# Three value tiles first in the neighbourhood attention, and the gate's mix beside the key products in the RWKV layer

## The chip, the cores and the metric

The kernel runs on one core of one Trainium2 chip. The metric is the device time of one execution in microseconds (us). Before the change, three runs took 2551.04, 2552.61 and 2557.27 us; the median is 2552.61.

## What is computed

The reference is a diffusion transformer of four layers with two streams: 256 latent tokens `x` and 256 context tokens `xc`, each token 1024 wide. Each layer is modulation, a mixer, a gated residual with a layer norm, and an MLP with squared ReLU. The mixers are attention with axial rotary positions (layers 0 and 3), neighbourhood attention (layer 1) and a bidirectional RWKV-7 (layer 2). Cut to the two places that matter here:

```python
# layer 1, neighbourhood attention
q, k, v = jnp.split(u @ wqkv, 3, axis=-1)        # u: latent or context tokens
# layer 2, RWKV
xx = _token_shift_centred(h)
xr, xw, xk, xv, xa, xg = [h + xx * p['mu'][j] for j in range(6)]
r = (xr @ p['wr']).reshape(hs)
k = xk @ p['wk']
v = (xv @ p['wv']).reshape(hs)
w = p['w0'] + tanh(xw @ w1) @ w2                 # shortened
a = sigmoid(p['a0'] + (xa @ a1) @ a2)            # shortened
g = jax.nn.sigmoid(xg @ p['g1']) @ p['g2']
...
return (y * g) @ p['wo']
```

So the RWKV layer mixes `h` six times with its neighbours, once for each of six products. The gate `g` is used only at the layer's end.

## The kernel before

**Products.** Activations lie with the feature on the partitions, in eight tiles of 128 features by 512 tokens (context and latent tokens beside each other). A product of full precision is made of three matmuls on rounded halves: high weight by high activation (L430), high weight by low activation (L431), low weight by high activation (L432); for products that have the tokens on the partitions the same three are L479 to L481. A product of one weight tile (128 output features) is thus 8 x 3 = 24 matmuls of 512 columns. An activation is split by ACT, which rounds it to the high half, and DVE, which subtracts (`split`, L425).

**Weights.** `Stream` brings weight tiles of 512 KB in the order of the list `PLAN`: SP loads `wr`, ACT rounds it to `wh`, and DVE subtracts to get `wl` (L280), which I call the residue. `W.next` checks that the tile asked for is the next of `PLAN`, so a product that moves has to move in `PLAN` too. `W.depth` says how many tiles are split ahead. The engines work in order, and a scheduler with priorities decides the order of each engine's instructions before the launch.

**Neighbourhood attention** (`natten`). The layer's input for the latent tokens is late: its norm needs the end of the layer before (`centre`, `finish`). `opening` therefore runs some passes on the context tokens alone first, with `centre` and `finish` issued among them (`at`). Here the passes are two value tiles, `values(0)` and `values(1)`; their weights are kept, and `together` (L856 to L858) then does both tiles for the latent tokens. Tiles 2 and 3 follow for all tokens. In `finish`, ACT takes the square root `rs` of the variance product, DVE scales `zc`, ACT makes `hx`, and `split` makes the pair `h`.

**RWKV.** `mixer(j)` makes the mixed tiles of one of the six products when asked for, each by one DVE instruction (L1025) and one split. `low` is a product on eight such tiles, made as it goes. The order of the program is: the products for `r`, `low` of `w1`, of `a1` and of `g1` (whose sigmoid goes into `sig`), and then eight key products; three tiles of the next mix are asked for ahead of each `low`'s last instruction (`PM` = 3). From key 0 on, preparatory steps for the recurrent units run beside the products: `wps` (`gate_products`, L1177), `kss` (L1192), and in the end `AR` and `BK` on DVE, from which 32 small matmuls (`tps`, L1263) make the triangles. DVE and DMAs carry these to POOL, which solves them (L1290, L1292), and the result R (L1313) is needed by PE at L1322. Between the keys and R the values' products run.

Of the kernel before, what the change touches and what calls it, by code (L numbers as in the profile page):

```python
# [12 lines left out]
AF = mybir.ActivationFunctionType  # L13
# [23 lines left out]
def plan():  # L37

    g = []
    for i in range(DEPTH):  # L40
        if i % 3 == 0:
            a = i // 3
            g += [("att_wqkv", a, "T", 0, n) for n in (8, 9)]
            g += [("att_wqkv", a, "V", kh, 5) for kh in range(2)]
            g += [("att_wqkv", a, "T", 0, n) for n in range(8)]
            g += [("att_wo", a, "T", 0, n) for n in range(8)]
        elif i % 3 == 1:
            g += [("na_wqkv", 0, "V", kh, 8 + j) for j in range(4) for kh in range(2)]
            for c in range(8):
                g += [("na_wqkv", 0, "T", 0, 8 + c), ("na_wqkv", 0, "T", 0, c)]  # L50
            g += [("na_wo", 0, "T", 0, n) for n in range(8)]
        else:
            g += [("rw_wr", 0, "T", 0, n) for n in range(8)]
            g += [("rw_w1", 0, "L", 0, 0), ("rw_a1", 0, "L", 0, 0), ("rw_g1", 0, "T", 0, 0)]
            g += [("rw_wk", 0, "T", 0, n) for n in range(8)]
            g += [("rw_wv", 0, "V", kh, j) for j in range(4) for kh in range(2)]
            g += [("rw_wo", 0, "T", 0, n) for n in range(8)]
        for w, q in MLP_ORDER:
            if w == "1":
                g += [("mlp_w1", i, "T", 0, 8 * q + n) for n in range(8)]  # L60
            else:
                g += [("mlp_w2", i, "T", q, n) for n in range(8)]
    return g
# [130 lines left out]
def dit_kernel(ctx: ExitStack, tc: tile.TileContext, places, t_in, out, layers=DEPTH):  # L194
    nc = tc.nc
    pe, dve, pool, sp = nc.tensor, nc.vector, nc.gpsimd, nc.sync
    act = InOrder(tc, nc.scalar)
# [23 lines left out]
    def bank(p, n, name):  # L221
        return p.tile([128, 512], F32, tag="b", name=name)[:, 0:n]
# [69 lines left out]
    W = Stream()  # L292
# [168 lines left out]
        mm3(ps, w, h[KC - 1], 0, 512, KC - 1, False, True)  # L461
        return ps

    def gemm_v(h, parts, toks):

        out = []
        for x, t in enumerate(toks):
            if x % 2 == 0:
                ps_b = bank(ps_mm, 512, "vps")
            out.append(ps_b[:, (x % 2) * 256:(x % 2) * 256 + 256])  # L470
        for kh in range(2):
            wh, wl = parts[kh]() if callable(parts[kh]) else parts[kh]
            for x, t in enumerate(toks):
                ps = out[x]
                for k in range(4):
                    c = kh * 4 + k
                    sh, sl = h[c][:, 0, t * 128:(t + 1) * 128], h[c][:, 1, t * 128:(t + 1) * 128]
                    first, last = c == 0 and x % 2 == 0, c == 7 and x % 2 == 1
                    pe.matmul(ps, lhsT=sh, rhs=wh[:, k * 256:(k + 1) * 256], start=first, stop=False)  # L479
                    pe.matmul(ps, lhsT=sh, rhs=wl[:, k * 256:(k + 1) * 256], start=False, stop=False)  # L480
                    pe.matmul(ps, lhsT=sl, rhs=wh[:, k * 256:(k + 1) * 256], start=False, stop=last)  # L481
        return out
# [348 lines left out]
    def natten(i, h, gate, nrm, begun, ends):  # L831
        V = [k4("nV") for _ in range(4)]
        kept = {}

        def values(j, toks):
            def part(kh):
                def go():
                    if (j, kh) not in kept:
                        kept[j, kh] = W.next("na_wqkv", 0, "V", kh, 8 + j)
                    return kept[j, kh]  # L840
                return go

            def go():
                for t, ps in zip(toks, gemm_v(h(), [part(0), part(1)], toks)):
                    act.copy(out=V[t][:, j * 256:(j + 1) * 256], in_=ps)
            return go

        def together():

            ps = [bank(ps_mm, 512, "vps").rearrange("p (t d) -> p t d", t=2) for _ in range(2)]  # L850
            for c in range(KC):
                for j in range(2):
                    vh, vl = (w[:, (c % 4) * 256:(c % 4) * 256 + 256] for w in kept[j, c // 4])
                    for t in range(2):
                        sh, sl = (h()[c][:, y, t * 128:(t + 1) * 128] for y in range(2))
                        pe.matmul(ps[j][:, t], lhsT=sh, rhs=vh, start=c == 0 and t == 0, stop=False)  # L856
                        pe.matmul(ps[j][:, t], lhsT=sh, rhs=vl, start=False, stop=False)
                        pe.matmul(ps[j][:, t], lhsT=sl, rhs=vh, start=False, stop=c == 7 and t == 1)  # L858
            for j in range(2):
                for t in range(2):  # L860
                    act.copy(out=V[t][:, j * 256:(j + 1) * 256], in_=ps[j][:, t])

        opening(begun, (0, 1), lambda cnd: [values(0, TOKS[1]), values(1, TOKS[1])] if cnd else [together], at=(0, 0))
        kept.clear()
        values(2, range(4))()
        values(3, range(4))()
        kept.clear()
        h = h()
# [93 lines left out]
    def rwkv(i, hx, gate, nrm, begun, ends):  # L962
# [143 lines left out]
        made[1](PM)  # L1106
        act.activation(out=lora[:, 0], in_=ps, func=AF.Tanh)
        ps = low("rw_a1", "L", made[1])
        made[2](PM)
        act.copy(out=lora[:, 1], in_=ps)  # L1110
        ps = low("rw_g1", "T", made[2])
        made[3](PM)
        act.activation(out=sig, in_=ps, func=AF.Sigmoid)
        m = made[3](KC)
        W.limit = PLAN.index(("rw_wo", 0, "T", 0, 0))
        W.depth = 2

        def keys(c):
            def go():
                if c == 9:  # L1120
                    W.depth = 1
                keep(c, 1, gemm(W.next("rw_wk", 0, "T", 0, c), m, ALL))
                if c == 7:
                    made[4](PM)
            return go
# [36 lines left out]
        def prep(c):  # L1162
# [5 lines left out]
            def gate_products():  # L1168
                q["sg"], q["ag"] = [], []
                wa = sml.tile([128, 2, 128], F32, tag="wa", bufs=2, name="wa")  # L1170
                sp.dma_start(out=wa, in_=t_in["rws"][c, :, 0:2])
                todo = []
                for x, (key, bias) in enumerate((("sg", "w0"), ("ag", "a0"))):
                    for d in range(2):
                        sl = slice(64 * d, 64 * d + 64)
                        ps = bank(ps_s if x else ps_mm, 512, "wps")
                        pe.matmul(ps, lhsT=wa[sl, x], rhs=lora[sl, x], start=True, stop=True)  # L1177
                        t = tmp(512 if x else 520, key)
                        q[key].append(t)
                        dst = t  # L1180
                        if x == 0:
                            dve.memset(b8(t)[:, :, 0:1], 0.0)
                            dst, ps = b8(t)[:, :, 1:65], b8(ps)
                        todo.append(dict(out=dst, in_=ps, bias=C(bias, "rw")[:, d, c:c + 1]))
                sigmoids(todo)
            out.append(gate_products)

            def unit_k():
# [610 lines left out]
```

## Time and profile before

| | |
|---|---|
| median of three runs | 2552.61 us |
| the profiled execution itself | 2547.62 us |
| its span, first to last instruction | 2545.2 us |
| PE busy | 2448.7 us, 96% |
| DVE busy | 1664.0 us, 65% |
| ACT busy | 1188.7 us, 47% |
| POOL busy | 209.2 us, 8% |
| mean granted clock | 0.987 |

The profiled execution is 5.0 us shorter than the median. Times in the rows below count from its first instruction. "PEclk" is the clock granted to PE as a share of its full 2.4 GHz. In a timeline, consecutive equal instructions are one row with their count (x3), and the bracket at a row's end is the idle time just before it on the engine, with the instruction that ended it.

### The profile page before, as it was taken

How to read it: one execution, taken by the hardware profiler on the slowest of the kernel's cores; microseconds unless marked ns; L12 is line 12 of the kernel's file. 1: busy time of each engine (PE TensorE's matmuls, PEld its weight loads, DVE VectorE, ACT ScalarE, POOL GpSimd, SP SyncE). 2: the span in 40 equal slices, each digit the busy share in tenths (PEclk: the TensorE clock that was granted, in tenths of full speed). 3: DMA queues.
4: the chain of work that ended last, by engine and by line, in shares of the span. 5: the costliest groups of instructions: out<-in, count | busy, mean ns of one | idle time of the engine just before them, and what ended most of it. 6: DMA issues, size and time to landing. Idle time of an engine off the chain costs nothing. (4 is left out here: it accounts for less than half of the span.)

```text
span 2545.2 us, 53184 instructions
## 1 busy us (share of the span) xinstructions
PE 2448.7 (96%) x22337; PEld 2085.8 (82%) x22337; DVE 1664.0 (65%) x3087; ACT 1188.7 (47%) x2226; POOL 209.2 (8%) x383
## 2 busy tenths in 40 slices
PE   8999999999999999999889799899999999998998
PEld 5779888889766988888867677778898888998997
DVE  4567777775566777787786565673567663766555
ACT  3555443244566543334555444544362343465644
POOL 0002000002000110000202112211020000121000
PEclk9999999999999999999999999999999999999999
DMA  8432556642211245665132311210336654223553
GB/s 337 166 127 75 182 189 192 207 157 88 69 55 58 88 152 182 207 205 176 60 112 77 80 28 33 41 20 15 143 107 216 206 184 126 93 68 115 175 184 98
DMA packets 158415, 324.11 MB, mean 127 GB/s; under 512 B 77393, under 2 KB 80993, under 8 KB 158177
## 3 DMA queue, kind: packets, MB, share of 16 engines
q1 hardware_dynamic: 158176, 320.73, 39.8%
q8 instruction: 175, 2.87, 0.5%
q14 instruction: 64, 0.52, 0.1%
HBM read 310.71 MB, written 9.97 MB: 126 GB/s over the span
## 5 line engine op out<-in xcount | busy, mean ns | idle before, releaser
L430 PE MATMUL mm<-h,wh 128*128 128x512 f32 (+1 forms) x1472 | 515.5, 351 | 6.1 <-ACT h L180 4.7
L432 PE MATMUL mm<-h,wl 128*128 128x512 f32 (+1 forms) x1472 | 511.6, 348 | 1.1 <-DVE wl L280 1.1
L280 DVE TENSOR_TENSOR wl<-wr,wh 128x1024 fp32r<-128x1024 f32 x363 | 442.7, 1227 | 103.5 <-ACT wh L180 77.9
L431 PE MATMUL mm<-h,wh 128*128 128x512 f32 (+1 forms) x1472 | 510.0, 347 | 0.3 <-DVE h L425 0.2
L180 ACT CAST wh<-wr 128x1024 fp32r<-128x1024 f32 x363 | 373.8, 1049 | 261.7 <-DVE wl L280 89.2
L430 PE MATMUL mm<-f,wh 128*128 128x512 f32 (+1 forms) x1168 | 397.6, 340 | 0.0
L432 PE MATMUL mm<-f,wl 128*128 128x512 f32 (+1 forms) x1168 | 397.6, 340 | 0.0
L431 PE MATMUL mm<-f,wh 128*128 128x512 f32 (+1 forms) x1168 | 397.0, 340 | 0.0
L430 PEld LDWEIGHTS mm<-h,wh 128*128 128x128 f32 x1472 | 279.4, 190 | 50.0 <-issue 8.8
L432 PEld LDWEIGHTS mm<-h,wl 128*128 128x128 f32 x1472 | 279.8, 190 | 37.1 <-issue 3.0
L431 PEld LDWEIGHTS mm<-h,wh 128*128 128x128 f32 x1472 | 279.8, 190 | 34.5 <-issue 2.8
L431 PEld LDWEIGHTS mm<-f,wh 128*128 128x128 f32 x1168 | 221.6, 190 | 24.7
L430 PEld LDWEIGHTS mm<-f,wh 128*128 128x128 f32 x1168 | 221.6, 190 | 24.5
L432 PEld LDWEIGHTS mm<-f,wl 128*128 128x128 f32 x1168 | 221.6, 190 | 24.2
L180 ACT ACTIVATE relu<-mm 128x512 f32<-128x512 f32 (+1 forms) x146 | 72.5, 497 | 360.4 <-PE mm L432 360.3
L425 DVE TENSOR_TENSOR f<-sqr,f 128x512 fp32r<-128x512 f32 (+1 forms) x146 | 82.4, 567 | 210.4 <-ACT f L180 210.4
L492 DVE SCALAR_TENSOR_TENSOR x<-mm,gate,x 128x256 f32<-128x256 f32 x280 | 127.3, 480 | 128.5 <-PE mm L432 128.3
L544 POOL TENSOR_SCALAR x<-zc,cs 128x256 f32<-128x256 f32 x88 | 86.0, 990 | 1302.9 <-DVE zc L575 1302.9
L387 DVE SCALAR_TENSOR_TENSOR mwt<-mwt,srow 128x1024 f32<-128x1024 f32 x144 | 175.8, 1221 | 8.3 <-DMA mwt<-in_mwr_dram 6.9
L387 DVE SCALAR_TENSOR_TENSOR mpr<-mwt,srow 128x1024 f32<-128x1024 f32 x112 | 136.7, 1220 | 0.5
L430 PE MATMUL mm<-o,wh 128*128 128x256 f32 (+1 forms) x400 | 120.1, 302 | 0.3 <-ACT o L180 0.2
L432 PE MATMUL mm<-o,wl 128*128 128x256 f32 (+1 forms) x400 | 119.9, 300 | 0.1
(292 smaller groups left out, 4317.9 us busy)
## 6 DMA issues: line engine op xcount, KB each, us to landing
wr<-in_gw_dram SPq DMA_DIRECT2D x363, 512.0 KB, 3.7
mwt<-in_mwr_dram SPq DMA_DIRECT2D x144, 512.0 KB, 4.3
mwt<-in_mw_dram SPq DMA_DIRECT2D x48, 512.0 KB, 5.4
srow<-srow_d SPq DMA_DIRECT2D x6, 512.0 KB, 4.1
nab<-in_nab_dram SPq DMA_DIRECT2D x8, 384.0 KB, 3.3
rk<-rk_d SPq DMA_DIRECT2D x6, 512.0 KB, 5.1
rk_d<-rkp SPq DMA_DIRECT2D x10, 256.0 KB, 2.2
x<-in_xt_dram SPq DMA_DIRECT2D x4, 512.0 KB, 10.2
```

The costliest lines, as they stand in the source:

```text
L180: x = f(*args, **kw)
L280: self.lo[self.done % len(self.lo)].tensor_tensor(out=lo, in0=t, in1=hi.bitcast(F32), op=ALU.subtract)
L387: dve.scalar_tensor_tensor(out=to, in0=t, scalar=1.0, in1=rw_["s"][cnd], op0=ALU.mult, op1=ALU.mult, accum_out=m[:, cnd, r * 8 + c:r * 8 + ...
L425: eng.tensor_tensor(out=dst[:, 1, a:b], in0=src, in1=dst[:, 0, a:b].bitcast(F32), op=ALU.subtract)
L430: pe.matmul(ps, lhsT=st, rhs=hl[:, 0, a:b], start=first, stop=False)
L431: pe.matmul(ps, lhsT=st, rhs=hl[:, 1, a:b], start=False, stop=False)
L432: pe.matmul(ps, lhsT=wl[:, c * 128:(c + 1) * 128], rhs=hl[:, 0, a:b], start=False, stop=last)
L492: dve.scalar_tensor_tensor(out=xc(c)[:, a:b], in0=ps[:, a - base:b - base], scalar=gate[:, cnd, c:c + 1], in1=xc(c)[:, a:b], op0=ALU.mult, ...
L544: (eng or dve).tensor_scalar(out=dst, in0=src, scalar1=ca, scalar2=cb, op0=ALU.mult, op1=ALU.add)
```

## The change

In the neighbourhood attention three value tiles in place of two are done first for the context tokens, the norm's `finish` comes behind the second, and `together` does three tiles. Their accumulators come from the pools in `OPEN`. Tile 3 alone remains for all tokens at once.

In the RWKV layer the weight of `g1` moves in `PLAN` from ahead of key 0 to behind key 3. The eight mixed tiles of the gate are asked for two at a time behind the key products 0 to 3, and `low` of `g1` comes behind key 3. Its result is copied, and the sigmoid is taken in place in the batch of unit 1's sigmoids. Ahead of key 0, the key's mix follows `low` of `a1`. The condition `c == 9` that goes was never true.

```diff
--- before.py
+++ after.py
@@ -51,8 +51,10 @@
             g += [("na_wo", 0, "T", 0, n) for n in range(8)]
         else:
             g += [("rw_wr", 0, "T", 0, n) for n in range(8)]
-            g += [("rw_w1", 0, "L", 0, 0), ("rw_a1", 0, "L", 0, 0), ("rw_g1", 0, "T", 0, 0)]
-            g += [("rw_wk", 0, "T", 0, n) for n in range(8)]
+            g += [("rw_w1", 0, "L", 0, 0), ("rw_a1", 0, "L", 0, 0)]
+            g += [("rw_wk", 0, "T", 0, n) for n in range(4)]
+            g += [("rw_g1", 0, "T", 0, 0)]
+            g += [("rw_wk", 0, "T", 0, n) for n in range(4, 8)]
             g += [("rw_wv", 0, "V", kh, j) for j in range(4) for kh in range(2)]
             g += [("rw_wo", 0, "T", 0, n) for n in range(8)]
         for w, q in MLP_ORDER:
@@ -461,12 +463,12 @@
         mm3(ps, w, h[KC - 1], 0, 512, KC - 1, False, True)
         return ps
 
-    def gemm_v(h, parts, toks):
+    def gemm_v(h, parts, toks, pool=None):
 
         out = []
         for x, t in enumerate(toks):
             if x % 2 == 0:
-                ps_b = bank(ps_mm, 512, "vps")
+                ps_b = bank(pool or ps_mm, 512, "vps")
             out.append(ps_b[:, (x % 2) * 256:(x % 2) * 256 + 256])
         for kh in range(2):
             wh, wl = parts[kh]() if callable(parts[kh]) else parts[kh]
@@ -832,7 +834,7 @@
         V = [k4("nV") for _ in range(4)]
         kept = {}
 
-        def values(j, toks):
+        def values(j, toks, pool=None):
             def part(kh):
                 def go():
                     if (j, kh) not in kept:
@@ -841,28 +843,27 @@
                 return go
 
             def go():
-                for t, ps in zip(toks, gemm_v(h(), [part(0), part(1)], toks)):
+                for t, ps in zip(toks, gemm_v(h(), [part(0), part(1)], toks, pool)):
                     act.copy(out=V[t][:, j * 256:(j + 1) * 256], in_=ps)
             return go
 
         def together():
 
-            ps = [bank(ps_mm, 512, "vps").rearrange("p (t d) -> p t d", t=2) for _ in range(2)]
+            ps = [bank(ps_mm, 512, "vps").rearrange("p (t d) -> p t d", t=2) for _ in range(3)]
             for c in range(KC):
-                for j in range(2):
+                for j in range(3):
                     vh, vl = (w[:, (c % 4) * 256:(c % 4) * 256 + 256] for w in kept[j, c // 4])
                     for t in range(2):
                         sh, sl = (h()[c][:, y, t * 128:(t + 1) * 128] for y in range(2))
                         pe.matmul(ps[j][:, t], lhsT=sh, rhs=vh, start=c == 0 and t == 0, stop=False)
                         pe.matmul(ps[j][:, t], lhsT=sh, rhs=vl, start=False, stop=False)
                         pe.matmul(ps[j][:, t], lhsT=sl, rhs=vh, start=False, stop=c == 7 and t == 1)
-            for j in range(2):
+            for j in range(3):
                 for t in range(2):
                     act.copy(out=V[t][:, j * 256:(j + 1) * 256], in_=ps[j][:, t])
 
-        opening(begun, (0, 1), lambda cnd: [values(0, TOKS[1]), values(1, TOKS[1])] if cnd else [together], at=(0, 0))
+        opening(begun, (0, 1), lambda cnd: [values(j, TOKS[1], OPEN[j + 2]) for j in range(3)] if cnd else [together], at=(0, 1))
         kept.clear()
-        values(2, range(4))()
         values(3, range(4))()
         kept.clear()
         h = h()
@@ -1106,20 +1107,19 @@
         made[1](PM)
         act.activation(out=lora[:, 0], in_=ps, func=AF.Tanh)
         ps = low("rw_a1", "L", made[1])
-        made[2](PM)
+        made[3](PM)
         act.copy(out=lora[:, 1], in_=ps)
-        ps = low("rw_g1", "T", made[2])
-        made[3](PM)
-        act.activation(out=sig, in_=ps, func=AF.Sigmoid)
         m = made[3](KC)
         W.limit = PLAN.index(("rw_wo", 0, "T", 0, 0))
         W.depth = 2
 
         def keys(c):
             def go():
-                if c == 9:
-                    W.depth = 1
                 keep(c, 1, gemm(W.next("rw_wk", 0, "T", 0, c), m, ALL))
+                if c < 4:
+                    made[2](2 * c + 2)
+                if c == 3:
+                    act.copy(out=sig, in_=low("rw_g1", "T", made[2]))
                 if c == 7:
                     made[4](PM)
             return go
@@ -1182,7 +1182,7 @@
                             dve.memset(b8(t)[:, :, 0:1], 0.0)
                             dst, ps = b8(t)[:, :, 1:65], b8(ps)
                         todo.append(dict(out=dst, in_=ps, bias=C(bias, "rw")[:, d, c:c + 1]))
-                sigmoids(todo)
+                sigmoids(todo + ([dict(out=sig, in_=sig)] if c == 1 else []))
             out.append(gate_products)
 
             def unit_k():
```

On PE, at the end of the context tokens' second pass, the order before is this (`vps` are value products, `pvar` is the variance product on which `finish` waits; L856 and L857 are `together`):

```order
L481 MATMUL vps_5692<-wh_5589,h_5461 128x256
L479 MATMUL vps_5692<-wh_5589,h_5467 128x256
L480 MATMUL vps_5692<-wl_5590,h_5467 128x256
L481 MATMUL vps_5692<-wh_5589,h_5467 128x256
L537 MATMUL pvar_5643<-s1_5623,cs_83 128x256
L856 MATMUL vps_5755<-wh_5243,h_5422 128x256
L857 MATMUL vps_5755<-wl_5244,h_5422 128x256
L856 MATMUL vps_5756<-wh_5559,h_5422 128x256
L857 MATMUL vps_5756<-wl_5560,h_5422 128x256
L479 MATMUL vps_5857<-wh_5693,h_5422 128x256
```

After the change (lines count two more there) a third pass of 48 products stands in between, and `pvar` in it:

```order
L482 MATMUL vps_5643<-wl_5590,h_5467 128x256
L483 MATMUL vps_5643<-wh_5589,h_5467 128x256
L481 MATMUL vps_5755<-wh_5644,h_5422 128x256
L482 MATMUL vps_5755<-wl_5645,h_5422 128x256
L483 MATMUL vps_5755<-wh_5644,h_5422 128x256
L481 MATMUL vps_5755<-wh_5644,h_5428 128x256
L539 MATMUL pvar_5706<-s1_5623,cs_83 128x256
L482 MATMUL vps_5755<-wl_5645,h_5428 128x256
L483 MATMUL vps_5755<-wh_5644,h_5428 128x256
```

What moved is `pvar`, four products into the new pass, and `together`, which now begins behind all of it.

On PE in the RWKV layer, the end of `a1` (`low_12158`) was followed by the gate's product (`low_12230`):

```order
L430 MATMUL low_12158<-mh_12200,wh_12090 128x512
L431 MATMUL low_12158<-mh_12200,wh_12090 128x512
L432 MATMUL low_12158<-mh_12200,wl_12091 128x512
L430 MATMUL low_12230<-mh_12208,wh_12152 128x512
L431 MATMUL low_12230<-mh_12208,wh_12152 128x512
L432 MATMUL low_12230<-mh_12208,wl_12153 128x512
L1177 MATMUL wps_12408<-lora_11513,wa_12398 128x512
L430 MATMUL low_12230<-mh_12213,wh_12152 128x512
L1177 MATMUL wps_12411<-lora_11513,wa_12398 128x512
```

It is now followed by key 0 (`mm_12268`), which runs on the next mixed tiles:

```order
L433 MATMUL low_12158<-mh_12200,wh_12090 128x512
L434 MATMUL low_12158<-mh_12200,wl_12091 128x512
L432 MATMUL mm_12268<-mh_12208,wh_12152 128x512
L433 MATMUL mm_12268<-mh_12208,wh_12152 128x512
L434 MATMUL mm_12268<-mh_12208,wl_12153 128x512
L1177 MATMUL wps_12356<-lora_11513,wa_12346 128x512
L432 MATMUL mm_12268<-mh_12213,wh_12152 128x512
L1177 MATMUL wps_12359<-lora_11513,wa_12346 128x512
```

The gate's product (`low_12475`) stands behind key 3 (`mm_12431`), with a `wps` of unit 1 in it:

```order
L432 MATMUL mm_12431<-mh_12244,wh_12376 128x512
L433 MATMUL mm_12431<-mh_12244,wh_12376 128x512
L434 MATMUL mm_12431<-mh_12244,wl_12377 128x512
L432 MATMUL low_12475<-mh_12294,wh_12425 128x512
L433 MATMUL low_12475<-mh_12294,wh_12425 128x512
L1177 MATMUL wps_12770<-lora_11513,wa_12760 128x512
L434 MATMUL low_12475<-mh_12294,wl_12426 128x512
L432 MATMUL low_12475<-mh_12299,wh_12425 128x512
L433 MATMUL low_12475<-mh_12299,wh_12425 128x512
```

So 24 products went from ahead of key 0 to ahead of key 4, and the two `wps` of unit 0 that stood among them are in key 0.

On DVE, the last key tiles before the change (`mh_12306` to `mh_12316`) are followed by residues of weights and by unit 0:

```order
L1025 SCALAR_TENSOR_TENSOR mix_12317<-xx_11524,cs_rw_11511,x_117 128x512
L425 TENSOR_TENSOR mh_12306<-mix_12307,mh_12306 128x512
L425 TENSOR_TENSOR mh_12311<-mix_12312,mh_12311 128x512
L425 TENSOR_TENSOR mh_12316<-mix_12317,mh_12316 128x512
L1530 MEMSET resets_12321 128x520
L280 TENSOR_TENSOR wl_12335<-wr_12156,wh_12334 128x1024
L1531 MEMSET resets_12321 128x8
L1182 MEMSET sg_12402 128x8
L1182 MEMSET sg_12406 128x8
L280 TENSOR_TENSOR wl_12367<-wr_12228,wh_12366 128x1024
L1203 SCALAR_TENSOR_TENSOR sg_12402<-resets_12321,sg_12402 128x520
L280 TENSOR_TENSOR wl_12429<-wr_12338,wh_12428 128x1024
```

After it (`mh_12244` is the last key tile) the gate's tiles come between them, beginning with `mix_12295` and `mh_12294`:

```order
L427 TENSOR_TENSOR mh_12239<-mix_12240,mh_12239 128x512
L1026 SCALAR_TENSOR_TENSOR mix_12245<-xx_11524,cs_rw_11511,x_117 128x512
L1530 MEMSET resets_12249 128x520
L1026 SCALAR_TENSOR_TENSOR mix_12295<-xx_11521,cs_rw_11511,x_114 128x512
L427 TENSOR_TENSOR mh_12244<-mix_12245,mh_12244 128x512
L1531 MEMSET resets_12249 128x8
L1026 SCALAR_TENSOR_TENSOR mix_12300<-xx_11521,cs_rw_11511,x_114 128x512
L282 TENSOR_TENSOR wl_12263<-wr_12094,wh_12262 128x1024
L427 TENSOR_TENSOR mh_12294<-mix_12295,mh_12294 128x512
L427 TENSOR_TENSOR mh_12299<-mix_12300,mh_12299 128x512
L1026 SCALAR_TENSOR_TENSOR mix_12337<-xx_11522,cs_rw_11511,x_115 128x512
L282 TENSOR_TENSOR wl_12305<-wr_12156,wh_12304 128x1024
```

What moved are the gate's mixes and splits: they stood ahead of the key tiles and now stand among the residues for keys 1 to 4.

## Rows read from the trace of the kernel before

**Rows 1.** The page, busy time of each engine, share of the span, instructions.
```profile
PE 2448.7 (96%) x22337; PEld 2085.8 (82%) x22337; DVE 1664.0 (65%) x3087; ACT 1188.7 (47%) x2226; POOL 209.2 (8%) x383
```

**Rows 2.** Busy time by stretch around the attention's values.
```profile
core 0: us, PE busy (x) PEld busy (x) DVE busy (x) ACT busy (x) POOL busy (x), PEclk, DMA share, GB/s
600.00:610.00 10.00, 6.53 (x37) 5.76 (x36) 7.63 (x14) 8.02 (x20) 6.42 (x7) 0.83 0.16 54
610.00:620.00 10.00, 10.00 (x86) 10.00 (x85) 1.08 (x3) 2.02 (x7) 1.10 (x2) 1.00 0.42 118
```

**Rows 3.** Timeline of PE from 600 to 642: start, duration, what, idle before.
```profile
600.51 0.28 PE L481 MATMUL vps<-wh,h 128*128 128x256 f32 x1
601.10 0.70 PE L537 MATMUL pvar<-s,cs 128*128 128x256 f32 x2 [0.31 <-DVE s L530]
604.96 0.39 PE L856 MATMUL vps<-wh,h 128*128 128x256 f32 x1 [3.16 <-ACT h L180]
...
606.21 0.42 PE L856 MATMUL vps<-wh,h 128*128 128x256 f32 x1
606.42 0.42 PE L857 MATMUL vps<-wl,h 128*128 128x256 f32 x1
...
641.31 0.40 PE L430 MATMUL mm<-h,wh 128*128 128x512 f32 x1
```

**Rows 4.** Timeline of ACT in the same stretch.
```profile
603.52 1.09 ACT L180 ACTIVATE hx<-zc,ab 128x256 f32<-128x256 f32 x2 [0.76 <-DVE zc L575]
604.52 0.70 ACT L180 CAST h<-hx 128x256 fp32r<-128x256 f32 x2
```

**Rows 5.** Timeline of DVE in the same stretch.
```profile
600.96 1.22 DVE L280 TENSOR_TENSOR wl<-wr,wh 128x1024 fp32r<-128x1024 f32 x1
...
605.20 0.95 DVE L425 TENSOR_TENSOR h<-hx,h 128x256 fp32r<-128x256 f32 x2
```

**Rows 6.** Busy time by stretch (columns as in rows 2), around key 0.
```profile
1320.00:1330.00 10.00, 6.87 (x23) 3.90 (x23) 10.00 (x17) 7.61 (x12) 0.00 (x0) 1.00 0.39 113
```

**Rows 7.** Timeline of DVE, key tiles and unit 0.
```profile
1318.99 2.08 DVE L1025 SCALAR_TENSOR_TENSOR mix<-xx,cs_rw,x 128x512 f32<-128x512 f32 x3
...
1322.79 2.08 DVE L1025 SCALAR_TENSOR_TENSOR mix<-xx,cs_rw,x 128x512 f32<-128x512 f32 x3
...
1328.57 1.90 DVE L425 TENSOR_TENSOR mh<-mix,mh 128x512 fp32r<-128x512 f32 x3
...
1354.18 0.69 DVE L1220 TENSOR_TENSOR BK<-BK,cc 128x512 f32<-128x512 f32 x1
```

**Rows 8.** Timeline of PE, keys, first triangles and the solver's result.
```profile
1323.13 0.39 PE L431 MATMUL mm<-mh,wh 128*128 128x512 f32 x1
1323.35 0.39 PE L432 MATMUL mm<-mh,wl 128*128 128x512 f32 x1
...
1331.04 0.39 PE L432 MATMUL mm<-mh,wl 128*128 128x512 f32 x1
...
1361.98 1.15 PE L1263 MATMUL tps<-AR,BK 64*64 64x64 f32 x32
...
1406.13 0.74 PE L1322 MATMUL pa<-R,TT 32*32 32x32 f32 x34 [3.91 <-DVE R L1313]
```

**Rows 9.** Timeline of POOL, the solver: first, two between, last.
```profile
1380.61 0.40 POOL L1290 TENSOR_TENSOR xw<-lane 128x15 f32<-128x15 f32 x1 [31.59 <-DMA lane<-dr]
...
1390.30 0.32 POOL L1292 TENSOR_TENSOR lane<-lane,xw 128x64 f32<-128x64 f32 x1
...
1392.62 1.16 POOL L1292 TENSOR_TENSOR lane<-lane,xw 128x55 f32<-128x55 f32 x1
...
1398.04 0.23 POOL L1292 TENSOR_TENSOR lane<-lane,xw 128x15 f32<-128x15 f32 x1
```

**Rows 10.** Timeline of DVE beside the solver.
```profile
1392.25 2.62 DVE L280 TENSOR_TENSOR wl<-wr,wh 128x1024 fp32r<-128x1024 f32 x2
```

**Rows 11.** Timeline of ACT before the solver.
```profile
1377.74 1.28 ACT L180 ACT_TABLE_LOAD   x1
```

## The prediction

> **What bounds the kernel now.** I read the page's busy times first: the tensor engine (PE) is busy for 2448.7 of 2545.2 us [rows 1], so only stretches in which it idles, or runs at the lower clock, can give time back; the number of matmuls is the same after the change. After it I read the table of busy time by stretch, and then the timelines of the two stages touched, engine by engine.
>
> In the neighbourhood attention's value stage PE is busy 6.53 of the 10 us from 600 to 610, at a granted clock of 0.83, and 10.00 of 10 in the next ten [rows 2]. The gap is one wait: the last value product of the context tokens starts at 600.51, the variance product at 601.10, and the first product of `together` at 604.96, after 3.16 us on ACT's `h` [rows 3]. The chain behind that wait is the square root on ACT, the scaled `zc` on DVE, `hx` at 603.52, the rounded `h` at 604.52 [rows 4], and the low half of `h` at 605.20 [rows 5]. After the gap PE's matmuls of 256 columns stand 0.21 us apart (606.21, 606.42 [rows 3]) in place of 0.12 (86 in 10 us [rows 2]): 1.2 instead of 2.4 GHz, by the mean of 0.83 for some 3.4 of the ten us.
>
> In the RWKV layer the owner changes. From 1320 to 1330 DVE is busy 10.00 of 10 and PE 6.87 [rows 6]: DVE makes mixed tiles in groups of three, 2.08 us of mixes and 1.90 of splits, and a group starts 3.8 us after the one before (1318.99, 1322.79) [rows 7]. PE waits for each group. The last group's splits start at 1328.57 and end at 1330.47 [rows 7], and the last matmul of key 0 starts at 1331.04 [rows 8]. Here a tile less on DVE ahead of key 0 is time.
>
> Farther on PE waits 3.91 us for R, the solver's result, at 1406.13 [rows 8]. R comes from a chain that starts with the triangles of units 0 and 1 (`tps`, 32 matmuls behind key 5 and as many behind key 6) and runs on POOL from 1380.61 to 1398.27 [rows 9]. What is gained in the keys passes this wall only if those triangles come earlier.
>
> **The attention, part by part.** The change brings a third pass of 48 matmuls on the context tokens ahead of `together`. At 0.12 us it is 48 x 0.12 = 5.76 us of work that needs nothing from the waiting chain, from 600.63 to about 606.4, and with the variance product inside it (0.35 to 0.70) to about 606.9. The variance product stands four matmuls into the pass, at 600.63 + 0.48 = 601.11, which is when its input was ready before (601.10 [rows 3]), so the chain starts no later. Its added item is one rounding of a weight tile (1.05 us) on ACT, ahead of `hx`; it needs a buffer that the weight residue (the low half of a weight tile) at 600.96 (1.22 us, to 602.18 [rows 5]) gives up. So `hx` starts at about 603.9 instead of 603.52, the first `h` is there at 605.0 and its low half at about 605.7 to 606.0: a microsecond before PE asks. Afterwards `together` eats a channel tile in 18 x 0.12 = 2.16 us, and ACT makes two in at most 1.09 + 0.70 = 1.8 [rows 4]. No wait is left, and with no gap I take the clock to stay up.
>
> Sum: 288 matmuls lie between 600.63 and the first product of the next stage at 641.31 [rows 3]. That is 40.68 us now, and 288 x 0.12 + 0.54 = 35.1 without gap and half clock: 5.6 us. From both sides: 7 us cannot be, since the gap with its half clock is all that PE loses there; at worst the wait is only halved and the half clock stays (about 2.5 us gained). I take 5.6, because the work put in exceeds the idle time. All stages behind are full of PE work (10.00 of 10, as in [rows 2]), so it should stay.
>
> **The RWKV layer.** Taken away ahead of key 0 are eight tiles of the gate's mix on DVE: 8 x 3.8 / 3 = 10.1 us. One weight residue (1.2) leaves the stretch too, and two new mixes (1.4) of the gate enter it ahead of the last key tile's split. Net some 10.4 us by counting the order through with these durations: key 0 ends at about 1320.9 in place of 1331.3. The gate's product is not saved: 24 matmuls of 512 columns at 0.227 us (1323.13, 1323.35 [rows 8]), 5.44 us, now stand between keys 3 and 4 with a `wps` of the next unit inside it (0.5).
>
> From key 0's end to unit 0's triangles at 1361.98 [rows 8] PE worked 30.7 us without a gap. With the gate's product and the `wps` that is 36.7, from 1320.9 to 1357.6. I add 0.2 for key 1, whose residue comes right behind the last key tile's split. So the triangles start at 1357.8: **4.2 us** earlier. From both sides: equal work counted at key 1's end gives 5.3, less than nothing is the solver's rival below, and all waits I could not resolve (key 3's residue has some 1.2 us to spare, the gate's weight 0.3 to 1, the `kss` product 0.1) take 1 to 3 us.
>
> What could eat it is DVE. It gets 16 instructions of the gate, 10.1 us, in keys 1 to 4. But it also begins its work there 10.4 us earlier. Even if it could fit none of them into idle time, its last product for unit 0's triangles would end where it did, at 1354.18 + 0.69 = 1354.9 [rows 7], 2.9 us before PE wants it. On ACT the added roundings are the same number, moved; its plain copy of the gate (0.6) precedes a table load and a sigmoid (1.9 together) that delay only a weight needed two keys later. On SP the loads of the gate's weight and of keys 4 to 6 now queue behind the load of `wa` and copies of finished keys; the gate's weight lands about 1328 and is wanted at 1339, key 5's lands at 1345 and is wanted at 1352. POOL's two clears change places. One table load of 1.28 us disappears at 1377.74 [rows 11]; I count nothing for it, as PE waits for R behind it anyway.
>
> Together 5.6 + 4.2 = 9.8 us: the profiled execution's 2547.62 becomes 2537.8. The median of the three runs shown is 2552.61, 5.0 above that execution; the same saving gives **2542.8 us**.
>
> **POOL's solver, against the trace.** Its 28 operations take 17.7 us, 0.63 each, though one that meets an idle DVE takes 0.32 (1390.30) and one at 1392.62 takes 1.16 [rows 9], beside a weight residue on DVE [rows 10]. At the short duration the chain would be 28 x 0.31 = 9.0 us shorter, and at the long one 28 x 0.51 = 14.3 longer. The DVE work beside it keeps its amount, so I leave it at 0.63. The Trainium skill (GPSIMD Engine Reference, section 1, Specifications) says that GpSimd shares its SBUF interfaces with VectorE and collides with DVE instructions that read two SBUF inputs. The trace agrees: the residue at 1392.25 reads two inputs, 1.16 against 0.32. By that rule the change could go wrong through a shift on DVE alone, and that is the rival with the other sign.
>
> **The rivals.** (1) Only the attention's part arrives: 2552.6 - 5.6 = 2547.0. For it: the slacks of 0.1 to 1.2 us in the keys, four places where one late residue stops PE, and DVE nearly full; against it, the 2.9 us before the triangles. (2) Only the RWKV part arrives, 2552.6 - 4.2 = 2548.4: the extra rounding waits for more than the residue at 602.18 and `h` slips behind 606.9, or the clock falls anyway. Against it, the microsecond to spare. (3) Neither: the triangles are on time but R is not, and `h` late: 2552.6. (4) Slower: POOL's 28 operations meet two-input DVE instructions throughout. It decides from a mean of 0.63 + 9.8 / 28 = 0.98 us on; at 1.14, near the row's 1.16, the time is 2542.8 + 14.3 = 2557.1. For it, that the table load's absence moves ACT and with it DVE's mixes against POOL; against it, that the same instructions lie there in about the same order. That the gate's tiles still precede the keys on DVE is ruled out by the new order.
>
> **How the numbers follow.** What a measurement here can tell from no change is about 0.3%, 7.7 us, so the bound is 2544.9. Forecast 0.55, with its own range from 2536 (half of POOL's possible gain) to 2546; rival 1 0.24; rival 2 0.09; rival 3 0.05; rival 4 0.07. Nine tenths of the forecast's case and a fifth of rival 1 lie under the bound: 0.55 faster. Slower by over 0.3% is rival 4 and a little of rival 3: 0.08. The remainder, 0.37, is no change. The range runs from 2536 to 2553, which takes in rivals 1 to 3 and leaves out rival 4.
>
> **What would show it.** Right: PE 10.00 of 10 from 600 to 610 at clock 1.00 with no wait on `h`, the next stage's first product 5 to 6 us earlier; key 0's last matmul ten microseconds earlier against what precedes it, no gap in keys 1 to 5, the first triangles 4 us earlier, and the wait on R as long as now with R 4 us earlier. Wrong: a wait on `h` behind the third pass, waits on residues or mixed tiles in keys 1 to 4 or in the gate's product, POOL's 28 operations longer than 20 us, or a granted clock under 1.00 in the keys.

## The result and the profile after

The changed kernel takes 2537.57 us (median of five runs, 2533.5 to 2539.37) beside 2551.04 us for the kernel before (median of five). The ratio is 0.994 with a 95% interval of 0.9923 to 0.9958: 15.3 us less, 10.7 to 19.6 by the interval (the two medians themselves differ by 13.5). In the second measurement, in experiment 1, the ratio is 0.9952 (0.9939 to 0.9964), 12.2 us less. I had forecast 9.8 us less: the sign and the places were right, the size was too small. The profiled execution took 2533.76 us, its span is 2531.4.

In the attention, this is PE from 600 to 610 us (columns as in [rows 2]):

```profile
600.00:610.00 10.00, 10.00 (x83) 9.89 (x82) 8.54 (x14) 8.54 (x21) 6.17 (x5) 1.00 0.20 54
```

The 6.53 of [rows 2] is 10.00, and the clock 1.00 in place of 0.83. The timeline of PE shows the variance product inside the third pass, the end of that pass, the first product of `together` (L858), and the next stage's first product:

```profile
601.45 0.59 PE L539 MATMUL pvar<-s,cs 128*128 128x256 f32 x2
...
607.03 0.28 PE L483 MATMUL vps<-wh,h 128*128 128x256 f32 x1
607.15 0.28 PE L858 MATMUL vps<-wh,h 128*128 128x256 f32 x1
...
635.95 0.40 PE L432 MATMUL mm<-h,wh 128*128 128x512 f32 x1
```

There is no bracket any more: `together` follows at the 0.12 us of the rest. On ACT and DVE the chain is as counted, with the added rounding (`wh`) between the square root `rs` and `hx`:

```profile
602.08 0.47 ACT L182 ACTIVATE rs<-pvar,epz 128x256 f32<-128x256 f32 x1 [0.38 <-PE pvar L539]
...
602.91 1.04 ACT L182 CAST wh<-wr 128x1024 fp32r<-128x1024 f32 x1
603.85 1.10 ACT L182 ACTIVATE hx<-zc,ab 128x256 f32<-128x256 f32 x2
```
```profile
605.45 0.95 DVE L427 TENSOR_TENSOR h<-hx,h 128x256 fp32r<-128x256 f32 x2
```

`hx` starts 0.33 us later than before (603.52 in [rows 4]). Of this, 0.24 are there already at `rs`, ahead of the rounding (602.08 here, 601.84 in the kernel before), so the rounding itself costs some 0.1. The first two `h` are whole at 605.45 + 0.95 = 606.40, while PE asks at 607.15. From `pvar` to the next stage it was 641.31 - 601.10 = 40.21 us [rows 3] and is 635.95 - 601.45 = 34.50.

In the RWKV layer these are the last key tile's split and the last product for the first triangles on DVE, and key 0's last matmul, the first triangles and R's first use on PE:

```profile
1311.83 0.69 DVE L427 TENSOR_TENSOR mh<-mix,mh 128x512 fp32r<-128x512 f32 x1
...
1342.67 0.68 DVE L1220 TENSOR_TENSOR BK<-BK,cc 128x512 f32<-128x512 f32 x1
```
```profile
1312.91 0.40 PE L434 MATMUL mm<-mh,wl 128*128 128x512 f32 x1
...
1350.32 1.15 PE L1263 MATMUL tps<-AR,BK 64*64 64x64 f32 x32
...
1393.34 0.74 PE L1322 MATMUL pa<-R,TT 32*32 32x32 f32 x34 [4.24 <-DVE R L1313]
```

The layer begins 6.9 us earlier than before (its first low product at 1286.81 in place of 1293.71). Counted from there, key 0's last matmul comes 11.2 us earlier (1312.91 in place of 1331.04 [rows 8]) and the first triangles 4.8 us earlier (1350.32 in place of 1361.98 [rows 8]). DVE's last product for the triangles ends at 1342.67 + 0.68 = 1343.35, 7.0 us before PE wants it. PE's waits between 1313.5 and the triangles are a single one; the answer lists waiter, releaser, sum, times and longest:

```profile
PE kss L1192 <- ACT ksq L182: 0.4, 1, 0.4
```

So behind key 0 PE waits for none of DVE's mixes of the gate.

To compare executions I use three stretches that every profile has: from `pvar` to the next stage's first product, from the first low product to the first triangles, and from these to R's first use (`pa`). Here they are, in us:

| execution | attention | (between) | keys | triangles to R |
|---|---|---|---|---|
| before | 40.21 | 652.40 | 68.27 | 44.15 |
| changed | 34.50 | 650.86 | 63.51 | 43.02 |

They gain 5.7, 4.8 and 1.1 us, 11.6 together. The spans differ by 13.8. The column "between" runs from the attention's end to the first low product, over products that the change leaves alone; 1.5 of the missing 2.2 us lie there. Experiment 1 comes back to it.

### The profile page after: what moved, and what is told of

It is laid out like the page before. It is cut to its first block, busy times and chain, and to the rows that moved or that the text cites. A ratio compares the mean times of both kernels' runs of the same rounds, so it can differ in the third digit from the quotient of the medians.

```text
span 2531.4 us, 53187 instructions
## 1 busy us (share of the span) xinstructions
PE 2442.0 (96%) x22337; PEld 2080.4 (82%) x22337; DVE 1662.2 (66%) x3087; ACT 1188.7 (47%) x2227; POOL 210.8 (8%) x383
## 5 line engine op out<-in xcount | busy, mean ns | idle before, releaser
L433 PE MATMUL mm<-f,wh 128*128 128x512 f32 (+1 forms) x1168 | 396.6, 340 | 0.0
```

Of the source, the lines that this page charges most:

```text
L433: pe.matmul(ps, lhsT=st, rhs=hl[:, 1, a:b], start=False, stop=False)
```

## The experiments

**1. Each part alone, and both kernels again.** The first kernel has only the diff's hunks for the value tiles (`gemm_v`, `values`, `together`, `opening`), the second only those for `PLAN` and the RWKV layer; the other two have no edit.

> Only the attention's part of the change (three value tiles first, finish behind the second); the RWKV layer as before. Theory: this part saves the wait on h and the half clock behind it, 5.4 to 5.6 us, whatever happens later, so the time is that of before less 5.5 and the profile shows no wait on h between 600 and 610. Rival: part of the 3 to 4 us by which the whole change did better than forecast belongs here (a clock that stays up in later stages), and the time falls by 8 or more.

> Only the RWKV part (the gate's tiles and product behind the keys); the attention as before. Theory: the first triangles come 4.7 us earlier against the layer's first low product, the solver's result R 4.7 to 5.8 us, and the time falls by about 5. Rival: the part is worth 8 us or more, since the solver and the values behind the keys get shorter as well (the table load that goes, POOL against DVE).

> The changed kernel once more, for a second profiled execution. Theory: the two parts are worth 10.3 us together, and what the first profile showed beyond that (1.4 us at 1248 to 1251 and 1.4 at 1463 to 1466, where the kernel before ran at half clock and the changed one did not) belongs to single executions: in this profile such stretches lie elsewhere, and the time is 10 to 13 us below before. Rival: the stretches are missing at the same two places again, and the difference is 13 us or more each time.

> The kernel before once more, for a second profiled execution. Theory: half-clock stretches at 605.9 to 609.4 and 1305.9 to 1311.5, which follow long waits, are there again or nearly; those at 1248 and 1463 are not both there. Rival: all four are there.

| kernel | ratio to before | attention | (between) | keys | triangles to R |
|---|---|---|---|---|---|
| attention only | 0.9975 (0.9963 to 0.9987) | 34.50 | 650.87 | 67.41 | 43.77 |
| RWKV only | 0.9979 (0.9970 to 0.9987) | 40.20 | 650.87 | 63.51 | 43.07 |
| changed, again | 0.9952 (0.9939 to 0.9964) | 34.50 | 651.43 | 63.47 | 43.05 |
| before, again | 0.9997 (0.9987 to 1.0008) | 40.89 | 652.41 | 67.41 | 43.87 |

Of 2549.24 us, the median of before in this group, the ratios are 6.4, 5.4 and 12.2 us: the parts add up. The three stretches say the same, and each follows its own part only. A rival of 8 us or more from one part is outside the RWKV part's interval (7.6 at most). The attention's interval reaches 9.4, so the times alone do not rule it out there; its own stretch gains 5.7 to 6.4, and the stretch between is 1.5 us shorter in that kernel.

That stretch holds the first of the two places that I had named (1248 and 1463). In both executions of before PE works at half clock there, from 1247.7 and from 1249.9; in the changed kernel the place as far behind the attention's end is at full clock (columns as in [rows 2]; the third figure from the end is the clock):

```profile
1247.70:1251.10 3.40, 3.40 (x16) 3.40 (x17) 1.72 (x3) 1.35 (x2) 0.00 (x0) 0.50 0.55 154
```
```profile
1242.30:1245.70 3.40, 3.40 (x28) 3.35 (x29) 1.71 (x3) 1.86 (x4) 0.00 (x0) 1.00 0.43 154
```

The changed kernel's second execution has half clock a little earlier, from 1235.8 to 1242.6. The second place, 1463 to 1466, is at half clock in one execution of before only. So part of my theory holds: such stretches lie elsewhere in another execution, and the time is 12.2 us below before, not 13 or more. For the stretch between it is not shown. In all fifteen profiles of this document, the four executions with both parts in their old order take 652.4 us; of the eleven others nine take 650.9 to 651.4, each part alone among them, and two take 652.4. Whether the change itself is worth 1.0 to 1.5 us there stays open.

Single executions differ in one more place, the recurrence. One row for it, from R's first use to the first `wo` product, in the second execution of before and in the second of changed (the first ones took 396.6 and 396.4 us, both at 0.97):

```profile
1406.90:1807.50 400.60, 365.53 (x9812) 306.49 (x9812) 233.06 (x494) 188.62 (x434) 72.57 (x222) 0.95 0.19 41
```
```profile
1394.70:1786.80 392.10, 356.88 (x9812) 299.05 (x9812) 232.90 (x494) 188.30 (x434) 71.87 (x222) 0.98 0.20 43
```

The same 9812 PE instructions take 392.1 to 400.6 us as the mean granted clock goes from 0.98 to 0.95, with as large a difference within a kernel (4.0 and 4.3) as between the kernels. In the first pair of executions it explains nothing (396.6 and 396.4), in the second 8.5 of the 20.9 us between the spans. A profile's span is therefore no measure of this change; the stretches are. The half clock of the attention was there again in before (0.74 on the mean in the ten us from 600, against 0.83), and the one at 1305.9 to 1311.5 was not: the keys' stretch has a mean clock of 0.95 in the first execution of before and of 1.00 in the second, which is the 0.9 us between 68.27 and 67.41.

**2. The gate's tiles ahead of the keys again.**

```diff
         ps = low("rw_a1", "L", made[1])
+        made[2](KC)
         made[3](PM)
```

> The changed kernel, but the gate's eight mixed tiles are made ahead of the key's again; its product stays behind key 3. Theory (DVE's tiles ahead of key 0 are what PE waits for): from the first low product to the first triangles it takes 63.5 + 10.1 = 73 to 74 us, more than in the kernel before (67.4 to 68.3), and the time goes back to that of before or just over. Rival (the product's new place on PE is what saves): 63.5 as in the changed kernel.

The time went back to 0.9989 (0.998 to 0.9998) of before, and the keys' stretch to 76.9 us, 13.4 more than in the changed kernel; I had expected 10.1 more. PE waits ahead of key 0 in one row:

```profile
1312.44 0.80 PE L432 MATMUL mm<-mh,wh 128*128 128x512 f32 x1 [7.59 <-ACT mh L182]
```

The place of the product alone saves nothing; the tiles' place does. But the sum is not the one that I had expected. PE's waits in the stretch are 16.2 us, 10.7 more than in the changed kernel: 7.7 more on mixed tiles, and 3.0 more on roundings and residues of weights and other results. Its busy time is 60.62 us as against 57.95, 2.7 more, since PE runs at half clock from inside that wait on (0.52 on the mean from 1307 to 1317). One reason for the late weights is that ACT must wait for a buffer before it rounds one, since eight tiles more live beside the keys. Its waits, in the same stretch:

```profile
ACT wh L182 <- PE mm L433: 11.9, 4, 4.7
```

**3. The gate's product behind key 1.**

```diff
-            g += [("rw_wk", 0, "T", 0, n) for n in range(4)]
+            g += [("rw_wk", 0, "T", 0, n) for n in range(2)]
...
-                if c < 4:
-                    made[2](2 * c + 2)
-                if c == 3:
+                if c < 2:
+                    made[2](4 * c + 4)
+                if c == 1:
```

> The changed kernel with the gate's product behind key 1, its tiles made four beside each of keys 0 and 1. Theory: DVE cannot make them in so short a time, its eighth tile is there some 12.5 us after the last key tile and PE waits for it 1 to 3 us, so the first low product to the first triangles takes 64.5 to 66.5 us. Rival (the place behind the keys does not matter, as DVE has time): 63.5.

64.46 us, just below what the theory gave, but not in its way. PE waits nowhere in the gate's product, which starts at 1320.16, and its waits in the whole stretch are 3.9 us, as against 5.5 in the changed kernel; the only new one is 0.63 us on key 1's residue. What is longer is PE's busy time (60.30 as against 57.95), at a lower clock ahead of key 1, where the changed kernel has 1.00:

```profile
1296.80:1306.80 10.00, 8.66 (x20) 5.17 (x20) 9.46 (x16) 4.33 (x8) 0.00 (x0) 0.66 0.16 52
```

So the waits speak for the rival: four tiles beside a key are no visible hindrance. What the stretch would be at full clock was not measured. The time (0.9938, 0.9923 to 0.9953) cannot be told from the changed kernel's.

**4. The a1 product moved as well.**

```diff
...
-        made[1](PM)
+        made[3](PM)
         act.activation(out=lora[:, 0], in_=ps, func=AF.Tanh)
-        ps = low("rw_a1", "L", made[1])
-        made[3](PM)
-        act.copy(out=lora[:, 1], in_=ps)
...
+                if c <= 1:
+                    made[1](4 * (c + 1))
+                if c == 1:
+                    act.copy(out=lora[:, 1], in_=low("rw_a1", "L", made[1]))
+                if 1 < c <= 3:
+                    made[2]({2: 4, 3: 8}[c])
```

> The changed kernel with the a1 product moved too, behind key 1 with its tiles made four beside each of keys 0 and 1, and the gate's four beside each of keys 2 and 3. Theory: eight more tiles leave the stretch in which PE waits for DVE, which is worth 5.4 us of PE work at most; DVE is busy 55.9 of the 63.5 us, so part of it comes back as waits: 59 to 61.5 us from the first low product to the first triangles, 2 to 4.5 less than in the changed kernel. Rival: DVE is full there, residues and unit 0 come late, and it stays at 62 to 64.

63.69 us, the rival's: nothing is gained (0.9944, 0.9929 to 0.9958). PE is busy 58.47 of the 63.70 us, and its waits only lie elsewhere, several of them on late weights and tiles in the gate's product at 1334.0 to 1341.1. Of the two other places tried, neither gains anything; more were not tried.

**5. The table load ahead of unit 1's sigmoids.** I had counted nothing for the load that goes [rows 11]. The first kernel meant to bring it back did not:

```diff
-                    act.copy(out=sig, in_=low("rw_g1", "T", made[2]))
+                    act.activation(out=sig, in_=low("rw_g1", "T", made[2]), func=AF.Sigmoid)
...
-                sigmoids(todo + ([dict(out=sig, in_=sig)] if c == 1 else []))
+                sigmoids(todo)
```

> The changed kernel with the gate's sigmoid taken at once from its product, not in the batch of unit 1's sigmoids; nothing is left out. Theory: this brings back the table load ahead of unit 1's sigmoids, and the stretch from the first triangles to R goes from 43.0 back to 43.8 (what the kernel before has without a half clock), the stretch ahead stays at 63.5. Rival: PE waits for R anyway, the stretch stays at 43.0.

Its stretch to R was 43.13, but no table load stands ahead of unit 1's sigmoids in its trace: no exponential follows the gate's sigmoid before them. So this run decides nothing. The second moves the sigmoid itself behind unit 1:

```diff
-                sigmoids(todo + ([dict(out=sig, in_=sig)] if c == 1 else []))
+                sigmoids(todo + ([dict(out=sig, in_=sig)] if c == 2 else []))
```

> The changed kernel with the gate's sigmoid in the batch of unit 2's sigmoids, so that a table load stands ahead of unit 1's sigmoids again, behind the keys, as in the kernel before (taking the sigmoid at once from its product had not brought it back). Theory: the load shifts ACT's and with it DVE's mixes by 1.28 us against POOL, and the stretch from the first triangles to R goes from 43.0 to 43.2 in the changed kernel to 43.8, POOL's solver from 17.1 to 17.7. Rival: the two wps fewer behind the keys or something else sets it, and the stretch stays at 43.0 to 43.2.

The load is back:

```profile
1366.59 1.28 ACT L182 ACT_TABLE_LOAD   x1
1367.88 1.27 ACT L182 ACTIVATE sg<-wps,cs_rw 128x512 f32<-128x512 f32 x2
```

The stretch to R went from 43.02 to 43.68 us, and POOL's solver from 17.06 (1368.86 to 1385.92) to 17.94 (1369.18 to 1387.12). The keys' stretch stayed at 63.51. The time was 0.9965 (0.9952 to 0.9978). The solver starts no later against the triangles (18.35 us behind them, 18.54 in the changed kernel), so the delay is inside it. The rows show where it begins: the sigmoids `sg` come later, so DVE's scan of them runs beside POOL's second operation, in the changed kernel

```profile
1367.08 2.37 DVE L1203 TENSOR_TENSOR_SCAN sg<-resets,sg 128x520 f32<-128x520 f32 x2
1369.54 0.64 POOL L1292 TENSOR_TENSOR lane<-lane,xw 128x15 f32<-128x15 f32 x1
```

and with the load

```profile
1368.60 2.37 DVE L1203 TENSOR_TENSOR_SCAN sg<-resets,sg 128x520 f32<-128x520 f32 x2 [1.11 <-ACT sg L182]
1369.93 1.06 POOL L1292 TENSOR_TENSOR lane<-lane,xw 128x15 f32<-128x15 f32 x1
```

That is 0.42 of the solver's 0.88 us; the rest lies in other rows, such as one of 128x60 that takes 0.63 in place of 0.30. The other profiles agree: in the six with this load ahead of unit 1's sigmoids the second operation takes 1.03 to 1.06 us and the solver 17.7 to 17.9, in the nine without it 0.64 at most and 17.0 to 17.4. The stretch to R follows in five of the six (43.68 to 44.15, as against 43.02 to 43.29). In before with a1's tiles read (experiment 6) it is 43.26 with the load, as the steps behind the solver were shorter there. So the load that the change takes away was on the path to R, through POOL, and is worth some 0.65 us in this pair.

**6. The keys without the gate's mix.** Two versions, each in both kernels, leave the gate's mix out: the tiles of a1 are read in its place, or POOL copies the layer's input into the tiles.

```diff
         made = [mixer(j) for j in (1, 4, 5, 2, 3)]
+        made[2] = made[1]
```
```diff
                 while len(made) < n:
+                    if j == 5:
+                        t = pair("mh", F32R)
+                        pool.tensor_copy(out=t, in_=hx[0])
+                        made.append(t)
+                        continue
```

> The changed kernel without the gate's eight mixes and splits: its product reads the tiles of a1 instead (left out: the gate's own mix). Theory: beside keys 1 to 4 DVE has room for them, so they cost next to nothing there: 62.5 to 63.5 us from the first low product to the first triangles, as against 63.5. Rival: DVE is the bound there too, and without 10.1 us of its work the stretch falls to 60 or less.

> The kernel before without the gate's eight mixes and splits: its product reads the tiles of a1 (left out: the gate's own mix). Theory: ahead of key 0 each tile on DVE is time on the path, so the stretch from the first low product to the first triangles falls by 9 to 10.1 us, from 67.4 to 57.5 to 58.5. Rival: PE's work is the bound once they are gone, and it falls by 5 or less.

> The changed kernel, the gate's eight tiles copied by POOL from the layer's input when they are asked for, not mixed and split (left out: the gate's own mix); buffers live as long as in the changed kernel, which the version reading a1's tiles had spoilt. Theory: beside keys 1 to 4 DVE has room for the mixes, so without them the stretch from the first low product to the first triangles is 62.5 to 63.5 us, as against 63.5. Rival: DVE holds the keys up there, and the stretch falls to 61 or less.

> The kernel before with the same edit (left out: the gate's own mix). Theory: without the mixes ahead of key 0 PE is bound by its own work and the other tiles, as in the changed kernel: 62 to 64 us from the first low product to the first triangles, as against 67.4. Rival: each tile of 1.27 us is still on the path, and the stretch falls by 9 to 10 us to 57.5 to 58.5.

| kernel | keys | mean clock at its lowest |
|---|---|---|
| changed, a1's tiles read | 70.13 | 0.73 (1317 to 1322) |
| before, a1's tiles read | 63.30 | 0.50 (1325 to 1330) |
| changed, POOL copies | 69.01 | 0.68 (1319 to 1329) |
| before, POOL copies | 66.11 | 0.67 (1305 to 1315) |

With the mix left out altogether, before takes 63.30, as the changed kernel does with it (63.51). That was the rival's number, a fall of 4.1 us. Its way there is mixed: PE waits only 2.8 us in the sum, as against 5.5 in the changed kernel, and the clock falls, to 0.50 and 0.82 in the ten us from 1325, which costs some 3.4 us. At full clock it would be near 60 (63.30 - 3.4, an estimate), between the theory and the rival. My 57.5 to 58.5 had forgotten that PE has 58 us of work in this stretch.

The changed kernel got slower in both versions, which no theory had said. In the first, a1's tiles live until the gate's product, and the roundings of weights wait for buffers that a key before gives back:

```profile
1323.50 1.04 ACT L182 CAST wh<-wr 128x1024 fp32r<-128x1024 f32 x1 [5.38 <-PE mm L433]
```

In the second, PE waits 2.1 us for a weight's rounding ahead of key 1, and half clock follows; in before with POOL's copies PE waits 6.6 us for splits on DVE in the low products. So these three kernels say nothing on what the mixes cost. That they cost PE nothing in their new place was not shown by leaving them out; it stands on the changed kernel's own profile, where PE waits 0.4 us behind key 0 and on nothing of DVE.

## Why the prediction came out as it did

**The attention's wait.** Forecast 5.6 us. The stretch fell from 40.21 to 34.50, 5.7; against the other executions with the old order (40.89, 40.20) it is 6.4 and 5.7, as the half clock behind the wait lasts longer or shorter. The chain came out within 0.3 us at each step. The price was that of one execution's half clock, which is the small end.

**The DVE chain ahead of key 0.** Forecast: key 0 ends 10.4 us earlier. From the first low product to key 0's last matmul it is 37.33 us in the first execution of before, 36.45 in the second and in the kernel with the attention's part alone, and 26.10 and 26.08 in the two of the changed kernel: 10.4 without the half clock, 11.2 with it.

**The keys.** Forecast 4.2 us. Measured 4.8 against the profile that the forecast was made from, 3.9 against the other executions. Right, and the experiments show its two halves: tiles back ahead, and it is lost (76.9); tiles gone from ahead of key 0, and it is had (63.30, with a stretch at a lower clock in it).

**Behind the keys: the step that failed.** "One table load of 1.28 us disappears at 1377.74 [rows 11]; I count nothing for it, as PE waits for R behind it anyway." The wait for R is no cover here, since R itself comes sooner: 0.75 to 1.1 us from the triangles to R, of which the load, by the kernel that brings it back, is 0.65. In the first pair of executions 0.6 of the 1.1 us is the solver and 0.45 the steps behind it, which no run explains. What I had for a rival with the other sign, POOL against a moved DVE, acted with this sign: the scan on DVE, not a residue, moved off POOL's operation.

**The sum.** The forecast 2542.8 started from a median of 2552.61 for before; with five runs it is 2551.04. With the stretches it is 5.7 + 4.8 + 1.1 = 11.6 us against the first execution of before and 6.4 + 3.9 + 0.85 = 11.2 against the second, and 12.2 and 15.3 by the two measurements, whose intervals (9.2 to 15.6 and 10.7 to 19.6) both hold it. Of the 1.4 to 1.8 us that were missing in 9.8, about 0.9 is the path to R, and the rest the half clock, put too low in the attention and left out in the keys. A second term that I had put at nothing is the stretch between ("All stages behind are full of PE work"): it is 1.5 us shorter in the first pair and 1.0 in the second, and whether that belongs to the change is open. With it the first pair has 13.1 us and the second 12.2. What the first measurement shows beyond that has no stretch of its own; executions of one kernel differ by 4 us in the recurrence alone, and that it is this spread was not shown for the timed runs, only for the profiled ones.

**Slips in the working.** The solver has 30 operations, of 0.59 us on the mean, not 28 of 0.63. At the short duration 28 x 0.31 is 8.7, not 9.0, and half of that below 2542.8 is 2538, so the lower end of the range, 2536, does not come out of POOL's gain. The terms named for key 0 (10.1 + 1.2 - 1.4) add up to 9.9, not 10.4; the counted 10.4 is what was measured without the half clock.

**The rivals.** Parts that do not arrive: none, the two add up. The slower side, POOL at over 0.98 us an operation: its 30 operations took 17.06 to 17.39 us in the two executions of the changed kernel. The loads on SP landed in time, as forecast: PE waits for no weight behind key 0 in the changed kernel.

## What to carry to other kernels

Look for the stretch in which the bound changes hands: filling a wait with the engine's own work gave back here the wait and the half clock behind it, and work of the other engine that is moved out from ahead of it is worth only as much as the bound engine was waiting. When a late result sets a wait, an instruction ahead of it is not free because somebody waits for the result; ask whether it is on the way to that result. An experiment that leaves work out should leave the lifetimes of buffers alone, or it measures those.

## What was not expected

The same recurrence took 392.1 to 400.6 us at mean granted clocks of 0.98 to 0.95, with the same 9812 PE instructions each time. In the kernel that keeps a1's eight tiles longer, and does less work, the keys took 6.6 us more (70.13 against 63.51); a part of this is half clock. A POOL operation on 128x15 took 1.06 us beside DVE's scan and 0.64 otherwise, and so a table load on a third engine, ACT, changed when R was ready.
